# A hybrid decoder layer on one core: the merge takes the token chunks in the order 0, 1, 2 instead of 2, 0, 1, and the attention takes its token tiles in the order 0, 1, 2, 5, 4, 3, 7, 6

## The chip, the cores and the metric

The kernel runs on one core of one Trainium2 chip. The metric is the device time of one execution in microseconds (us), the median of several runs. Three runs of the kernel before gave 1844.86, 1845.64 and 1847.42 us.

## What is computed

One layer over 1024 prompt tokens and 8 sample tokens, with 1024 channels, everything in float32. The part that matters here is its second half, cut from the reference:

```python
# oa: output of the gated delta rule (mixer A); qb, kb, vb: queries, keys, values of mixer B
logits = einsum(qg, k_sel) * HD_B ** -0.5         # 8 query heads, 2 groups of keys and values
p  = softmax(where(valid, logits, -inf))          # at most 256 keys for each query, causal
ob = einsum(p, v_sel)
mix = sigmoid(ga) * (oa @ w_out_a) + sigmoid(gb) * (ob @ w_out_b)
h   = x + mix @ w_o
hn  = rms_norm(h, norm2_g)
y   = h + square(relu(hn @ w_up)) @ w_down
```

The first half (projections, delta rule, the choice of keys, the sample tokens' attention) stands ahead of it and is the same in both kernels.

## The kernel before, in words

The tokens are cut in two ways. The dense products work on three **chunks**: chunk 0 is token tiles 0 to 2 (384 columns), chunk 1 is tiles 3 to 5 (384 columns), chunk 2 is tiles 6 and 7 and the 8 sample tokens (264 columns). The attention works on eight **tiles** of 128 tokens, each in two groups `n` of four heads. Tile t looks at t + 1 blocks of 128 keys, so tile 0 has one block of work and tile 7 has eight.

Activations lie with channels on partitions. A dense product with one block of weights is a unit of 12 matmuls (four blocks of 128 input channels, three products each, since both operands are kept as a high and a low part), or 24 where two weight blocks feed one output. A block `wc` is 256 KB: SyncE (SP) issues its load, ScalarE writes its high part, VectorE (even number) or GpSimd (odd number) its low part.

`rest()` runs six chains side by side, and a scheduler turns them into one fixed order of instructions on each engine:

- The logit chain takes the groups (tile, n) in the order of the list `groups`: load of `q3`, rotation (`ro`, `qr`), transposition by TensorE (`ptq`), split into `qS`, logits `pat` by TensorE, VectorE's mask and maximum (`lg`, `st`), ScalarE's exponential. It is at most two groups ahead of the value chain.
- The value chain transposes for each group the reciprocal sums (`prr`) and the probabilities (`ptp`), splits them into `ph` (ScalarE) and `pl` (VectorE), multiplies with the values into `po`, and writes the scaled result `rb` to `obd` in DRAM.
- The merge chain first runs `mix_a` (the product with `w_out_a` for all three chunks, which doesn't need the attention), then `merge([j])` for each chunk j in `FIRST`, each as soon as the chunk's tiles are done, and last the merge of `REST`. A merge loads `ob` from `obd` (tiles `ld`), runs 8 units with `w_out_b` (`pdn<-ob`; VectorE makes `gb` and `ga`, ScalarE and GpSimd split the result into `mix`), then 8 units of 24 matmuls with `w_o` (`pdn<-mix`; VectorE adds into `hT`).
- The pool chain waits for all tiles and for the last `mix` of `FIRST`, closes the attention's buffers and opens those of the last stage; only then can the merge of `REST` begin, and `hn`, `ssq` and the root (`rst`, `rs`) of the chunks in `FIRST`.
- The MLP chain begins behind the merge of `REST`, and takes the chunks in the order `FIRST + REST`.

In the kernel before `FIRST, REST = [2, 0], [1]`: the two large tiles 7 and 6 are attended to first, beside `mix_a`; then tiles 0, 1, 2, while chunk 2 is merged; then tiles 5, 4, 3, while chunk 0 is merged; and chunk 1 is the `REST` whose merge stands alone ahead of the MLP.

Of the kernel before, what the change touches and what calls it, by code (L numbers as in the profile page):

```python
# [27 lines left out]
C_AQ, C_AZ, C_AB, C_BQ, C_BK, C_IQ, C_IK, C_GA = 0, 1536, 2048, 2056, 2568, 2824, 3336, 3408  # L28
WB = (5, 4)
LG = 9  # L30
FIRST, REST = [2, 0], [1]
XO = (0, 1, 2, 3, 4, 5, 6, 7, 8)
KVO = ([0, 1], [2, 3], [4, 5], [6, 7], [8])
IQO = (2, 3, 4, 5, 6, 7, 8)
# [12 lines left out]
class Event:  # L47
    t = None
# [80 lines left out]
def program(ctx, tc, I, O, dbg=None, upto=99):  # L129
# [1459 lines left out]
    def rest():  # L1589
# [12 lines left out]
        G.affine_select(cmask[:, P:], cmask[:, P:], pattern=[[-1, P]], compare_op=OP.is_ge, fill=NEG, base=0,  # L1602
                        channel_multiplier=1)
        chunks = FIRST + REST
        groups = [(t, n) for t in (7, 6, 0, 1, 2, 5, 4, 3) for n in range(2)]
        ev_lg, ev_pv = {g: Event() for g in groups}, {g: Event() for g in groups}
        front = {}

# [162 lines left out]
    if upto > 3:  # L1771
        rest()
# [80 lines left out]
```

## Time and profile before

| | before |
|---|---|
| median of 3 runs | 1845.64 us (1844.86 to 1847.42) |
| profiled execution, own time | 1847.76 us |
| its span in the trace | 1845.6 us |
| mean granted TensorE clock | 0.985 |
| TensorE matmul busy | 1767.7 us, 96% |
| VectorE, ScalarE, GpSimd busy | 1082.6, 813.0, 633.9 us |
| attention, mix_a and merges | about 794 to 1121 us of the span |
| MLP | 1121 to 1842 us |

The span is the time in the trace from the first to the last instruction. The profiled execution's own time is 2.2 us longer than its span, and 2.1 us above the median of the runs. Busy times are those of the matmuls as the profile models them.

### The profile page before, as it was taken

The numbers are of one execution on the slowest core, as the hardware profiler recorded it, in microseconds if no ns is written. First come the engines' busy times: TensorE is split into PE (matmuls) and PEld (weight loads), VectorE is DVE, ScalarE is ACT, GpSimd is POOL, SyncE is SP. The second block draws the span as 40 slices with busy tenths as digits, with TensorE's granted clock in tenths as the row PEclk, the third lists the DMA queues.
The fourth block names the chain that finished last, engine by engine and source line by source line (L and its number), as shares of the span: only waits on it lengthen the run. The fifth ranks groups of instructions, "written<-read, shape, count | busy, mean of one in ns | idle before, by whom it ended". The sixth has DMA issues, their size and how long they took to land. (4 is left out here: it accounts for less than half of the span.)

```text
span 1845.6 us, 32353 instructions
## 1 busy us (share of the span) xinstructions
PE 1767.7 (96%) x11796; PEld 1702.1 (92%) x11796; DVE 1082.6 (59%) x2871; ACT 813.0 (44%) x1865; POOL 633.9 (34%) x774
## 2 busy tenths in 40 slices
PE   6998979899999998989899989999999999999999
PEld 6998979789998998979789889999999999999999
DVE  8777767998889797358889685223232323231322
ACT  5456665465688542246677544222213131313130
POOL 5433235712332345231453665221212131213130
PEclk9999989999999998999999999999999999999999
DMA  6434463314443452663564552111111111111112
GB/s 215 130 106 153 141 216 108 92 56 119 135 149 113 147 166 87 199 219 115 177 173 139 179 159 86 52 41 52 46 51 48 46 47 46 46 52 41 52 29 93
DMA packets 160143, 199.27 MB, mean 108 GB/s; under 512 B 29648, under 2 KB 107464, under 8 KB 159976
## 3 DMA queue, kind: packets, MB, share of 16 engines
q1 hardware_dynamic: 155696, 183.57, 32.4%
q0 software_dynamic: 4288, 13.64, 2.5%
q8 instruction: 93, 1.52, 0.3%
q14 instruction: 66, 0.54, 0.1%
HBM read 149.51 MB, written 47.73 MB: 107 GB/s over the span
## 5 line engine op out<-in xcount | busy, mean ns | idle before, releaser
L86 PE MATMUL pdn<-hn,wc 128*128 128x384 f32 (+1 forms) x2304 | 362.0, 319 | 0.0
L86 PE MATMUL pdn<-u,wc 128*128 128x384 f32 (+1 forms) x2304 | 361.3, 318 | 0.0
L86 PEld LDWEIGHTS pdn<-hn,wc 128*128 128x128 f32 x2304 | 360.4, 188 | 0.3
L86 PEld LDWEIGHTS pdn<-u,wc 128*128 128x128 f32 x2304 | 360.1, 188 | 0.0
L86 DVE TENSOR_TENSOR hT<-hT,pdn 128x384 f32<-128x384 f32 (+1 forms) x216 | 110.5, 512 | 248.4 <-PE pdn L86 245.6
L86 PE MATMUL pdn<-xn,wu 128*128 128x384 f32 (+1 forms) x1440 | 253.0, 329 | 1.4 <-ACT z L86 1.4
L86 PEld LDWEIGHTS pdn<-xn,wu 128*128 128x128 f32 x1440 | 229.6, 193 | 8.2 <-issue 3.8
L86 DVE SCALAR_TENSOR_TENSOR r<-pdn,rs 128x384 f32<-128x384 f32 (+1 forms) x96 | 49.4, 516 | 273.5 <-PE pdn L86 273.4
L86 POOL TENSOR_TENSOR u<-r,u 128x384 fp32r<-128x384 f32 (+1 forms) x96 | 89.9, 937 | 274.9 <-ACT u L86 248.3
L86 PE MATMUL pa<-xn,wu 128*128 128x384 f32 (+1 forms) x864 | 157.7, 330 | 0.3 <-ACT a L86 0.3
L86 PEld LDWEIGHTS pa<-xn,wu 128*128 128x128 f32 x864 | 139.8, 193 | 2.7 <-ACT a L86 0.9
L86 ACT ACTIVATE r<-r 128x384 f32<-128x384 f32 (+1 forms) x96 | 47.1, 492 | 174.0 <-DVE r L86 173.3
L86 ACT ACTIVATE jka<-sc,nf 128x512 bf16<-128x512 f32 (+3 forms) x124 | 101.4, 820 | 37.8 <-DVE nf L86 26.7
L86 PE MATMUL pdn<-mix,wc 128*128 128x384 f32 (+1 forms) x576 | 95.0, 321 | 8.1 <-ACT mix L86 3.7
L86 PEld LDWEIGHTS pdn<-mix,wc 128*128 128x128 f32 x576 | 90.4, 188 | 11.8 <-ACT mix L86 4.5
L86 DVE SCALAR_TENSOR_TENSOR a<-u,cw,a 128x384 f32<-128x384 f32 (+1 forms) x108 | 73.3, 679 | 9.7 <-ACT a L86 8.4
L86 POOL TENSOR_TENSOR wu<-wu_4r,wu 128x512 fp32r<-128x512 f32 x32 | 41.7, 1303 | 89.7 <-ACT wu L86 83.3
L86 DVE TENSOR_SCALAR_CACHE_REDUCE jk<-sc,cf 128x768 bf16<-128x768 f32 (+1 forms) x62 | 66.3, 1072 | 1.5 <-ACT jka L86 1.5
L86 DVE SCALAR_TENSOR_TENSOR sc<-rl,wsg,sc 128x512 f32<-128x512 f32 (+1 forms) x70 | 51.3, 734 | 13.9 <-ACT rl L86 12.7
L86 PE MATMUL pqb<-wbq,xn 128*128 128x256 f32 (+1 forms) x432 | 59.3, 287 | 0.0
L86 PE MATMUL pdn<-oa,wc 128*128 128x384 f32 (+1 forms) x288 | 52.1, 329 | 7.0 <-DVE ga L86 6.5
L86 PEld LDWEIGHTS pqb<-wbq,xn 128*128 128x128 f32 (+1 forms) x432 | 55.2, 183 | 3.4
(888 smaller groups left out, 3234.2 us busy)
## 6 DMA issues: line engine op xcount, KB each, us to landing
wu_0r<-in_w_un SPq DMA_DIRECT2D x32, 256.0 KB
wu_4r<-in_w_un SPq DMA_DIRECT2D x32, 256.0 KB
gd<-g SPq DMA_DIRECT2D x32, 192.0 KB
ga<-gd SPq DMA_DIRECT2D x32, 192.0 KB
cqd<-a SPq DMA_DIRECT2D x24, 192.0 KB
xt<-in_x_prompt SPq DMA_DIRECT2D x8, 512.0 KB
obd<-rb SPq DMA_DIRECT2D x16, 256.0 KB
kvd<-kvt SPq DMA_DIRECT2D x8, 384.0 KB
```

The source lines that it names most:

```text
L86: return f(*a, **k)
```

## The change

Two lines. The first sets which chunks are merged beside the attention and which one is left for the end; the second sets the tiles' order so that each chunk's tiles are done when its merge is due.

```diff
-FIRST, REST = [2, 0], [1]
+FIRST, REST = [0, 1], [2]
...
         chunks = FIRST + REST
-        groups = [(t, n) for t in (7, 6, 0, 1, 2, 5, 4, 3) for n in range(2)]
+        groups = [(t, n) for t in (0, 1, 2, 5, 4, 3, 7, 6) for n in range(2)]
```

What the lines do to the order of instructions shows at three places. The first is TensorE's order where the attention begins, behind the first four units of `mix_a` (`pdn<-oa`: a unit of `mix_a`; `ptq`, `pat`, `prr`, `ptp`, `po`: the attention). Before:

```order
L86 MATMUL ptq<-ident,qr 128x128 x2
L86 MATMUL pdn<-oa,wc_10473 128x384 x12
L86 MATMUL pat<-kv,qS 128x512 x16
L86 MATMUL ptq<-ident,qr 128x128 x2
L86 MATMUL pdn<-oa,wc_10473 128x384 x12
L86 MATMUL pat<-kv,qS 128x512 x4
L86 MATMUL pdn<-oa,wc_10463 128x264 x12
L86 MATMUL prr<-ident,st 128x128 x4
L86 MATMUL ptp<-ident,lg 128x128 x8
L86 MATMUL pat<-kv,qS 128x512 x6
```

After the change the same place reads:

```order
L86 MATMUL ptq<-ident,qr 128x128 x2
L86 MATMUL pdn<-oa,wc_10475 128x384 x12
L86 MATMUL pat<-kv,qS 128x128 x8
L86 MATMUL ptq<-ident,qr 128x128 x2
L86 MATMUL pat<-kv,qS 128x128 x2
L86 MATMUL prr<-ident,st 128x128 x4
L86 MATMUL ptp<-ident,lg 128x128 x4
L86 MATMUL pat<-kv,qS 128x128 x6
L86 MATMUL ptq<-ident,qr 128x128 x2
L86 MATMUL po<-ph,kv 128x512
L86 MATMUL pdn<-oa,wc_10475 128x384 x12
L86 MATMUL po<-pl,kv 128x512
```

Tile 7's sixteen matmuls of 512 columns for one group have become tile 0's eight of 128 columns, and two units of `mix_a` that stood among the first two groups have moved behind them.

The second place is TensorE's order behind the last value product (`po`) of the attention. Before, seven pairs of units of 128x384 of chunk 0's `w_o` product follow it, fourteen units, of which eleven are shown:

```order
L86 MATMUL po<-pl,kv 128x512
L86 MATMUL pdn<-mix_12664,wc_13218 128x384 x12
L86 MATMUL pdn<-mix_12665,wc_13285 128x384 x12
L86 MATMUL pdn<-mix_12664,wc_13290 128x384 x12
L86 MATMUL pdn<-mix_12665,wc_13377 128x384 x12
L86 MATMUL pdn<-mix_12664,wc_13382 128x384 x12
L86 MATMUL pdn<-mix_12665,wc_13448 128x384 x12
L86 MATMUL pdn<-mix_12664,wc_13453 128x384 x12
L86 MATMUL pdn<-mix_12665,wc_13510 128x384 x12
L86 MATMUL pdn<-mix_12664,wc_13515 128x384 x12
L86 MATMUL pdn<-mix_12665,wc_13587 128x384 x12
L86 MATMUL pdn<-mix_12664,wc_13592 128x384 x12
```

After the change five pairs are left (of chunk 1), and then the merge of `REST` begins, on 264 columns:

```order
L86 MATMUL po<-pl,kv 128x512
L86 MATMUL pdn<-mix_12693,wc_13373 128x384 x12
L86 MATMUL pdn<-mix_12694,wc_13439 128x384 x12
L86 MATMUL pdn<-mix_12693,wc_13444 128x384 x12
L86 MATMUL pdn<-mix_12694,wc_13505 128x384 x12
L86 MATMUL pdn<-mix_12693,wc_13510 128x384 x12
L86 MATMUL pdn<-mix_12694,wc_13574 128x384 x12
L86 MATMUL pdn<-mix_12693,wc_13579 128x384 x12
L86 MATMUL pdn<-mix_12694,wc_13632 128x384 x12
L86 MATMUL pdn<-mix_12693,wc_13637 128x384 x12
L86 MATMUL pdn<-mix_12694,wc_13707 128x384 x12
L86 MATMUL pdn<-ob,wc_13712 128x264 x6
```

Four units of 128x384 have moved from behind the attention's end to ahead of it, and the sixteen outputs of the `REST` merge are 264 columns wide instead of 384.

The third place is SP's queue behind the last write of the attention's result (`obd<-rb`), with the loads of `ob` for `REST` (`ld<-obd`), of the residual (`hT<-in_xT`) and of weights (`wc`). Before:

```order
L1672 DMA obd<-rb 512x1x128
L216 DMA wc52r<-in_w_o 128x512
L216 DMA wc53r<-in_w_o 128x512
L216 DMA wc56r<-in_w_b 128x512
L1529 DMA ld<-obd 64x2x384 x2
L216 DMA wc50r<-in_w_o 128x512
L229 DMA hT_14009<-in_xT 128x1536 x2
L216 DMA wc54r<-in_w_o 128x512
L216 DMA wc55r<-in_w_o 128x512
L216 DMA wc57r<-in_w_b 128x512
L216 DMA wc58r<-in_w_b 128x512
L1529 DMA ld<-obd 64x2x384 x2
```

After the change:

```order
L1672 DMA obd<-rb 512x1x128
L216 DMA wc56r<-in_w_b 128x512
L1529 DMA ld<-obd 64x2x256
L216 DMA wc57r<-in_w_b 128x512
L1529 DMA ld<-obd 64x2x256 x3
L1532 DMA ld<-obs 128x2x8
L229 DMA hT_13979<-in_xT 128x1056 x2
L1529 DMA ld<-obd 64x2x256 x2
L1532 DMA ld<-obs 128x2x8
L216 DMA wc58r<-in_w_b 128x512
L216 DMA wc60r<-in_w_b 128x512
L1529 DMA ld<-obd 64x2x256 x2
```

The loads of `ob` stand closer behind the last write, with fewer loads of weights between them, and two small loads of the sample tokens' part (`obs`) have joined them.

## Rows read from the trace of the kernel before

**Rows 1.** The page's part 1: busy us, share of the span, instructions.

```profile
PE 1767.7 (96%) x11796; PEld 1702.1 (92%) x11796; DVE 1082.6 (59%) x2871; ACT 813.0 (44%) x1865; POOL 633.9 (34%) x774
```

**Rows 2.** Busy time by stretch: from:to, length, engines' busy us, PEclk, DMA share, GB/s.

```profile
809.30:825.00 15.70, 14.99 (x76) 11.49 (x77) 12.34 (x36) 9.88 (x17) 5.00 (x8) 1.00 0.73 242
825.00:896.00 71.00, 71.00 (x466) 65.84 (x465) 57.92 (x150) 44.26 (x96) 10.78 (x15) 1.00 0.43 130
896.00:925.00 29.00, 22.67 (x159) 19.97 (x158) 25.84 (x64) 19.87 (x52) 16.46 (x19) 1.00 0.65 192
925.00:964.00 39.00, 37.42 (x264) 33.59 (x263) 33.80 (x85) 27.41 (x59) 20.98 (x20) 1.00 0.65 183
964.00:1027.00 63.00, 63.00 (x409) 58.26 (x407) 53.95 (x123) 43.51 (x93) 22.93 (x20) 1.00 0.47 141
1027.00:1121.10 94.10, 84.42 (x461) 81.18 (x461) 75.54 (x98) 47.79 (x96) 65.98 (x51) 0.98 0.53 167
1130.00:1842.20 712.20, 712.18 (x4555) 711.86 (x4553) 195.42 (x355) 170.51 (x314) 169.40 (x158) 1.00 0.16 49
```

**Rows 3.** TensorE's waits, 896 to 925 us: us in total, times, longest.

```profile
PE pdn L86 <- DVE ga L86: 2.7, 1, 2.7
PE pat L86 <- DVE qS L86: 1.9, 2, 1.4
```

**Rows 4.** TensorE's waits, 1027 to 1121.1 us.

```profile
PE pdn L86 <- ACT mix L86: 3.7, 2, 2.0
...
PE pdn L86 <- ACT ob L86: 2.0, 1, 2.0
```

**Rows 5.** VectorE's groups by form, 873 to 925 us: count, busy us, mean ns, idle before.

```profile
L86 DVE TENSOR_TENSOR qS<-ptq,qS 64x256 fp32r<-64x256 f32 x11 | 4.7, 423 | 0.9 <-ACT qS L86 0.6
L86 DVE TENSOR_TENSOR ro<-q,tab 128x128 f32<-128x128 f32 x10 | 4.2, 446 | 0.2
...
L86 DVE TENSOR_TENSOR qr<-qr,ro 128x256 f32<-128x256 f32 x5 | 4.1, 819 | 0.1
...
L86 DVE CUSTOM_DVE_ANT_0 lg<-pat,cmask 128x128 f32<-128x128 f32 x8 | 2.2, 284 | 1.2 <-PE pat L86 1.2
```

**Rows 6.** ScalarE's groups by form, 873 to 925 us.

```profile
L86 ACT ACTIVATE qS<-ptq 64x256 fp32r<-64x256 f32 x10 | 3.7, 373 | 2.3 <-DVE qS L86 2.3
...
L86 ACT ACTIVATE lg<-lg,st 128x128 f32<-128x128 f32 x8 | 3.2, 399 | 0.4 <-DVE st L86 0.3
```

**Rows 7.** TensorE's timeline: start us, us, and the run of matmuls.

```profile
947.05 3.08 PE L86 MATMUL pdn<-mix,wc 128*128 128x264 f32 x24
...
1094.35 17.88 PE L86 MATMUL pdn<-mix,wc 128*128 128x384 f32 x101 [1.66 <-ACT mix L86]
```

**Rows 8.** VectorE's waits, 1027 to 1121.1 us.

```profile
DVE hT L86 <- PE pdn L86: 10.4, 6, 3.7
DVE ob L86 <- ACT ob L86: 6.1, 2, 3.3
```

**Rows 9.** VectorE's groups by form, 1027 to 1121.3 us.

```profile
L86 DVE SCALAR_TENSOR_TENSOR hn<-hT,g,hn 128x384 fp32r<-128x384 f32 x15 | 16.5, 1100 | 0.5 <-ACT hn L86 0.5
...
L86 DVE TENSOR_TENSOR ga<-ga,gb 128x384 f32<-128x384 f32 x8 | 7.5, 940 | 0.0
...
L86 DVE TENSOR_TENSOR wc<-wc56r,wc 128x512 fp32r<-128x512 f32 x1 | 1.5, 1500 | 0.0
...
L86 DVE TENSOR_TENSOR wc<-wc54r,wc 128x512 fp32r<-128x512 f32 x1 | 0.7, 693 | 0.2 <-ACT wc L86 0.2
```

**Rows 10.** The timeline's end: VectorE's last two additions into hT.

```profile
1838.03 0.43 DVE L86 TENSOR_TENSOR hT<-hT,pdn 128x264 f32<-128x264 f32 x1 [0.89 <-PE pdn L86]
...
1842.22 0.56 DVE L86 TENSOR_TENSOR hT<-hT,pdn 128x384 f32<-128x384 f32 x1 [1.55 <-PE pdn L86]
```

**Rows 11.** Busy time in stretches of 5 us around two of TensorE's waits; columns as in rows 2.

```profile
895.00:900.00 5.00, 2.30 (x18) 2.05 (x17) 2.76 (x9) 2.79 (x10) 2.15 (x3) 1.00 0.61 170
...
1065.00:1070.00 5.00, 4.67 (x18) 4.67 (x19) 3.77 (x4) 2.24 (x5) 4.96 (x4) 0.66 0.39 132
```

## The prediction

> **What bounds the kernel now.** The page's busy shares come first: TensorE's matmuls fill 96% of the span, VectorE 59%, GpSimd 34% [rows 1]. A change of order removes no matmul, so it can only move the other 4%, and only in the stretches whose order differs. I looked for these with busy times by stretch [rows 2]. The MLP, 712 us long, has 0.02 us of idle TensorE; it takes the same units in another order of chunks, so I count it as unchanged. The attention and the merges show three kinds of stretch. From 825 to 896 us (tiles 7 and 6 beside `mix_a`) and from 964 to 1027 us (tiles 5, 4, 3 beside merges) TensorE has no idle time at all. From 896 to 925 us, tiles 1 and 2 with few units beside them, it idles 29.00 − 22.67 = 6.3 us, while VectorE is busy 25.84 of 29 us; from 925 to 964 us another 1.6 us. And from the attention's end at 1027 us to the MLP at 1121 us it idles 94.10 − 84.42 = 9.7 us. The waits name the causes: in 896 to 925 us VectorE's `ga` (2.7 us) and `qS` (1.9 us) [rows 3]; behind the attention the last parts of `mix` (3.7 us) and of `ob` (2.0 us) [rows 4]. The reader is to see that a tile of few key blocks gives TensorE little to do and VectorE nearly as many instructions as a large tile, and that a merge without attention beside it waits for VectorE and what follows on it.
>
> **Start: the small tiles meet an empty pipeline.** Before, the attention starts on tile 7, and 809 to 825 us shows 0.7 us of idle time [rows 2]. After the change the order puts tile 0's groups there, eight matmuls of 128 columns each, and two units of `mix_a` move behind them. Go through TensorE's new order. Behind the first group's `pat` it has only a `ptq` until the second group's `qS` is made. That takes VectorE two `ro`, one `qr` and one `qS`, 2 × 0.45 + 0.82 + 0.42 = 2.1 us [rows 5], and ScalarE's half of `qS`, 0.37 us [rows 6], about 2.5 us together. The first `prr` then needs the group's last exponential, 0.40 us [rows 6], and VectorE's reciprocal behind it; with `prr` of the second group I put 0.6 us on each, 1.2 us. The third group's `ptq` needs four `lg` of 0.28 us and the two `ro` and the `qr`, 1.1 + 1.7 = 2.8 us [rows 5], of which the transpositions and six `pat` between cover about half: 1.4 us. Two `po` wait for their `pl`, as an estimate 0.5 us each. Sum 6.1 us, less the 0.7 us of before: **+5.4 us**. The lower bound: VectorE and ScalarE begin a group early enough that only the 2.1 us for the first `qS` remain, +1.4. The upper: tiles 0, 1 and 2 idle throughout as in 896 to 925 us, 0.22 us per us over some 45 us, +9.
>
> **Middle: the old holes close.** Tiles 5, 4, 3, 7, 6 now run beside the rest of `mix_a` and the merges of chunks 0 and 1. Both old stretches in which large tiles had merge units beside them show zero idle time [rows 2], so the 6.3 and 1.6 us go; I leave 1.5 us for new joints: **−6.4 us**, bounds −7.9 (all) and −2.4 (5.5 us remain, as the tail end of tile 2 is still short of cover).
>
> **End: a shorter cover.** TensorE's matmuls from the last value product to the MLP become fewer: four units of 12 on 384 columns move ahead of it, and 288 matmuls (96 of `w_out_b`, 192 of `w_o`) go from 384 to 264 columns. One of 384 takes 17.88 / 101 = 0.177 us, one of 264 takes 3.08 / 24 = 0.128 us [rows 7]. That is 48 × 0.177 + 288 × 0.049 = 22.6 us less there. None of it is a gain: the narrow units of chunk 2 and the wide ones of chunk 1 have changed places, and that work now stands beside the attention. If the idle time stayed at 9.7 us the stretch would be 94.1 − 22.6 = 71.5 us.
>
> VectorE's work hardly shrinks. It is 75.54 us there now [rows 2]. Two additions into `hT` go (2 × 0.56), sixteen `hT` and `gb` shrink by 0.56 − 0.43 = 0.13 us each, 2.1 us [rows 10], eight `ga` shrink in proportion to the columns, 7.5 × 120 / 384 = 2.3 us [rows 9]; two low parts of weights (1.5 us each, the dearer row) go, 3.0 us, two parts of `ob` give 0.5 us, and one more `hn` comes, 1.1 us [rows 9]. Net −7.9: 67.6 us. Its idle time there is 94.10 − 75.54 = 18.6 us, of which 10.4 us are waits for TensorE's `hT` units and 6.1 us waits for `ob` [rows 8]. The first kind is slack that goes when TensorE has less to do. If all the rest stays, 8.2 us, the stretch is 67.6 + 8.2 = 75.8 us, 4.3 us more idle TensorE than now. If the waits for `ob` go too, since its loads stand closer behind the last `obd` in SP's new queue, VectorE alone asks for 69.7 us, less than the 71.5 above: −1.8. I take **+3.0**, nearer the upper end, because the shorter cover (ten units, 10 × 12 × 0.177 = 21.2 us) must hold the write, the loads, the addition and both parts of `ob`, and fifteen `hn` of 1.1 us stand on VectorE in the same stretch.
>
> The price of VectorE's work there is not fixed. A low part of a weight block takes 0.69 us in one row and 1.50 in another of the same stretch, and `ga` takes 0.94 us [rows 9], while GpSimd is busy 65.98 of 94.10 us [rows 2]. The Trainium skill, GPSIMD Engine Reference, section Specifications, says that GpSimd's SBUF interfaces are shared with VectorE, with contention where VectorE reads two inputs from SBUF; these two rows agree, and by that rule the same GpSimd work in a shorter stretch would make VectorE's instructions dearer still. As a term it is bounded by rows: if the seventeen low parts and the sixteen `hn`, by the row of 1.1 us, become dearer by a fifth, that is 33 × 1.2 × 0.2 = 8 us on VectorE, and the end costs +11 instead of +3.
>
> **Tail.** The last unit is now one of 264 columns; its addition is 0.13 us shorter [rows 10]: −0.1 us.
>
> **Sum.** +5.4 − 6.4 + 3.0 − 0.1 = +1.9 us. The profiled execution's own time is 1847.76 us (span 1845.6), 2.1 us over the median of the runs, so the changed kernel would take 1849.7 us in such an execution and 1845.64 + 1.9 = **1847.5 us** as a median. A measurement here can tell about 0.2% (3.7 us) from no change, so this is a small loss that may not be seen.
>
> **Rivals.**
>
> *The end gets cheaper (faster, 0.17).* The wider merge of chunk 1 was what GpSimd and VectorE collided over; the narrow one collides less, and the fifteen or so low parts whose price lies near 1.5 us fall to the row of 0.69 us [rows 9]. That frees 15 × 0.81 = 12 us of VectorE, which then asks for 64 us, and TensorE, the bound again, idles about 4 us for the first `ob` and `mix` instead of 9.7: −5.7 in place of +3.0, sum −6.8, about 1838.8 us. For it: 0.69 occurs in this stretch. Against: GpSimd's share rises. It decides as soon as the mean low part costs less than about 0.9 us.
>
> *The end gets dearer (slower, 0.16).* The contention above, +11: sum +9.9, about 1855.5 us.
>
> *TensorE's clock falls between short bursts (slower, 0.14).* In 1065 to 1070 us, behind a wait of 2.0 us, the granted clock is 0.66, between its levels of 1.2 and 2.4 GHz; in 895 to 900 us, with a wait of 2.7 us in it, it stays 1.00 [rows 11]. A stretch of 5 us at 0.66 loses 5 × 0.34 = 1.7 us. If the start and the end, with more such waits, show four more of these, the sum is +1.9 + 6.8 = +8.7, about 1854.3 us. The Trainium skill, TensorE: Matmul & The Clock Gate, section HAM oscillation — how this bites in real kernels, describes this: bursts that are short against the waits between them start cold each time. The first row agrees with it, the second does not, hence the small chance.
>
> *The middle stays (slower, 0.11).* Tile 2 and the first large tiles find `mix_a`'s units spent by the small tiles, and only 2 of the 7.9 us go: sum +1.9 + 4.4 = +6.3, about 1851.9 us.
>
> **Chances and range.** The forecast has 0.42, spread from −5 to +5 us: 0.37 of it within 0.2% and 0.05 faster than that. Faster: 0.17 + 0.05 = 0.22. Within 0.2%: 0.37. Slower: 0.16 + 0.14 + 0.11 = 0.41. The forecast's own range is 1841 to 1851 us; the range of 8 in 10 takes in all of the slower cases but the far end and half of the faster one: 1839.5 to 1857 us.
>
> **What the new profile would show.** Right: in the first 25 us behind tile 0's first `pat`, 5 to 7 us of TensorE waits for `qS`, `st` and `pl`; from there to the last value product less than 2 us; then about 60 us of matmuls in a stretch of some 74 us, with waits for `mix` or `ob`, and VectorE busy over 90% of it. Wrong: an idle start as short as before (then the small tiles are covered and the sum turns negative), an end with idle time under 6 us or over 18, a granted clock under 0.9 over either stretch, or an MLP with idle time of its own.

## The result, and the profile after

The changed kernel takes 1859.29 us (median of 5 runs, 1857.16 to 1860.16) where the kernel before takes 1847.42 us on the same chip (5 runs, 1844.86 to 1851.11): 1.0063 times the time, 95% interval 1.0052 to 1.0073. That is 11.9 us slower. The forecast said 1.9 us, and the time lies above its range, which ended at 1857 us.

Busy time by stretch of the changed kernel, in the columns of [rows 2]; the attention's first tile starts at 809.4 us, its last value product ends at 1057 us, the MLP begins at 1133.2 us:

```profile
809.40:845.00 35.60, 32.46 (x188) 29.36 (x188) 27.73 (x90) 20.76 (x62) 10.06 (x15) 0.90 0.64 206
845.00:882.00 37.00, 36.77 (x237) 33.93 (x235) 28.22 (x76) 20.63 (x45) 8.38 (x9) 1.00 0.65 178
882.00:892.40 10.40, 5.16 (x21) 4.67 (x22) 6.05 (x12) 4.78 (x10) 5.92 (x6) 0.67 0.29 92
892.40:1057.00 164.60, 161.75 (x962) 149.80 (x961) 127.47 (x280) 102.59 (x199) 57.81 (x51) 0.99 0.46 133
1057.00:1133.20 76.20, 62.50 (x404) 58.80 (x403) 70.37 (x90) 42.03 (x88) 58.44 (x47) 0.96 0.53 159
1142.00:1854.10 712.10, 712.10 (x4567) 712.10 (x4566) 206.04 (x358) 165.64 (x315) 171.15 (x158) 1.00 0.16 49
```

The MLP is as long as before. Idle TensorE time is 3.1 us at the start (0.7 before), 0.2 + 5.2 + 2.9 = 8.3 us from there to the last value product (7.9 before), and 13.7 us behind it (9.7 before): 6.9 us more in all. And there is a second part that no idle time shows. From the first unit of `mix_a` to the MLP, TensorE does the same matmuls in both kernels (a few of their records are missing from each trace), but is busy longer:

```profile
794.06:1121.10 327.04, 304.45 (x1878) 279.89 (x1877) 268.00 (x567) 198.06 (x422) 151.44 (x143) 0.99 0.55 168
```

```profile
791.78:1133.20 341.42, 311.86 (x1869) 288.54 (x1868) 270.58 (x564) 197.79 (x419) 150.81 (x141) 0.96 0.53 158
```

The first row is the kernel before, the second the changed one: 7.4 us more busy time, at a mean granted clock of 0.96 instead of 0.99. The stretch as a whole is 14.4 us longer; ahead of it, where both kernels do the same, this profile of the changed kernel is 2.3 us shorter (the first unit of `mix_a` starts at 791.78 us instead of 794.06). Where the added busy time is spent shows in stretches of 5 us of the changed kernel, and in TensorE's timeline there:

```profile
815.00:820.00 5.00, 5.00 (x18) 4.50 (x18) 2.89 (x11) 2.62 (x10) 1.34 (x2) 0.50 0.78 263
...
885.00:890.00 5.00, 2.76 (x11) 2.46 (x12) 3.71 (x8) 3.44 (x8) 4.21 (x6) 0.55 0.30 95
...
1070.00:1075.00 5.00, 5.00 (x22) 5.00 (x21) 5.00 (x5) 2.97 (x7) 5.00 (x5) 0.68 0.34 88
1105.00:1110.00 5.00, 4.31 (x23) 4.10 (x24) 5.00 (x10) 2.92 (x6) 3.56 (x4) 0.73 0.49 148
```

```profile
812.26 0.44 PE L86 MATMUL pat<-kv,qS 128*128 128x128 f32 x2 [1.47 <-DVE qS L86]
813.34 0.73 PE L86 MATMUL prr<-ident,st 128*128 128x128 f32 x4 [0.64 <-DVE st L86]
...
816.96 4.01 PE L86 MATMUL pdn<-oa,wc 128*128 128x384 f32 x12
...
879.70 2.26 PE L86 MATMUL pdn<-oa,wc 128*128 128x384 f32 x12
887.24 1.12 PE L86 MATMUL prr<-ident,st 128*128 128x128 f32 x4 [5.28 <-DVE st L86]
```

A unit of `mix_a` that takes 2.26 us at 879.70 us takes 4.01 us at 816.96 us, in a stretch whose clock is 0.50, the lower of the two levels; ahead of it TensorE had waits of 1.47 and 0.64 us and short matmuls. The longest single wait, 5.28 us, is new: `prr` waits for `st` at 887.24 us. ScalarE's and VectorE's timelines say for what:

```profile
877.90 0.94 ACT L86 ACTIVATE ob<-ld 128x384 fp32r<-128x384 f32 x2 [1.20 <-issue]
885.12 0.94 ACT L86 ACTIVATE ob<-ld 128x384 fp32r<-128x384 f32 x2 [6.28 <-POOL ld L86]
885.97 0.92 ACT L86 ACTIVATE lg<-lg,st 128x768 f32<-128x768 f32 x1
```

```profile
885.68 0.78 DVE L86 TENSOR_TENSOR ob<-ld,ob 128x384 fp32r<-128x384 f32 x1 [6.66 <-ACT ob L86]
887.01 0.18 DVE L86 RECIPROCAL st<-st 128x4 f32<-128x4 f32 x1 [0.55 <-ACT lg L86]
```

ScalarE stands still 6.28 us in front of the second half of chunk 0's `ob`, which GpSimd has not added up yet. The last two loads of this half are issued behind other transfers at 877.63 us, and the addition starts at 883.29 us (timelines of SyncE and GpSimd):

```profile
877.63 1.23 SPq L1529 DMA_DIRECT2D ld<-obd  x2
883.29 1.80 POOL L86 TENSOR_TENSOR ld<-ld 128x768 f32<-128x768 f32 x1 [5.30 <-issue]
```

GpSimd is idle for 5.30 us ahead of it, and the profile names no releaser there; that it waits for these loads is read from the order of the program. Behind that `ob`, in the fixed order, wait the last exponential of tile 5's group and then VectorE's reciprocal, on which `prr` waits. ScalarE's orders (listed, without times) show the place. In the kernel before, the two halves stand apart, with attention work between them:

```
L86 ACTIVATE ob<-ld 128x264 x2
L86 ACTIVATE lg,st<-lg,st 128x256
L86 ACTIVATE wc_11633<-wc11r 128x512
L86 ACTIVATE qS<-ptq 64x2x128 x2
L86 ACTIVATE wc_11677<-wc12r 128x512
L86 ACTIVATE rb<-prr 128x512
L86 ACTIVATE ph<-ptp 128x512 x2
L86 ACTIVATE ob<-ld 128x264 x2
```

In the changed kernel all four conversions stand in a row, ahead of an exponential:

```
L86 ACTIVATE lg,st<-lg,st 128x768
L86 ACTIVATE ob<-ld 128x384 x4
L86 ACTIVATE lg,st<-lg,st 128x768
L86 ACTIVATE ph<-ptp 128x512
```

Behind the attention the waits are VectorE's low parts of weights first, then `mix` and a high part of a weight block; VectorE is busy 70.37 of 76.20 us there, and the wait for `hT` that led its idle time before is gone:

```profile
PE pdn L86 <- DVE wc L86: 5.3, 4, 2.3
PE pdn L86 <- ACT mix L86: 3.2, 2, 1.9
PE pdn L86 <- ACT wc L86: 2.9, 1, 2.9
```

### The profile page after: what moved, and what is told of

Same layout as the page of the kernel before. It is cut to its first block, busy times and chain, and to the rows that moved or that the text cites. A ratio compares the mean times of both kernels' runs of the same rounds, so it can differ in the third digit from the quotient of the medians.

```text
span 1857.5 us, 32361 instructions
## 1 busy us (share of the span) xinstructions
PE 1774.7 (96%) x11796; PEld 1710.0 (92%) x11796; DVE 1099.7 (59%) x2871; ACT 808.0 (44%) x1865; POOL 638.3 (34%) x774
## 4 chain that ended last, share of the span: by engine, by line
PE 47%; DVE 3%; issue 1%; POOL 1%; DMA 1%; ACT 0%; SPq 0%; DVEq 0%; ACTq 0%; POOLq 0%
PE pdn L86 43%; PE po L86 1%; PE ptp L86 1%; PE pat L86 1%; DVE hn L86 1%; DVE rst L86 0%; DMA ld<-obd 0%; DVE wc L86 0%; POOL ld L86 0%; PE prr L86 0%; DVE hT L86 0%; DVE rs L86 0%; DVE ga L86 0%; POOL ssq L86 0%; DVE gb L86 0%
## 5 line engine op out<-in xcount | busy, mean ns | idle before, releaser
L86 PE MATMUL pdn<-mix,wc 128*128 128x384 f32 (+1 forms) x576 | 98.9, 328 | 12.2 <-DVE wc L86 3.7
L86 DVE SCALAR_TENSOR_TENSOR sc<-rl,wsg,sc 128x512 f32<-128x512 f32 (+1 forms) x70 | 52.9, 757 | 11.6 <-ACT rl L86 10.5
L86 ACT ACTIVATE lg<-lg,st 128x128 f32<-128x128 f32 (+7 forms) x64 | 49.4, 773 | 21.6 <-DVE st L86 21.4
```

What stands on the lines that cost most here:

```text
L86: return f(*a, **k)
```

## Experiments

Each time is a median, taken on the same chip as runs of the kernel before; ratios are to those runs, with their 95% interval. The chip differs from one group of experiments to the next, so across groups ratios are compared and not times. Four things were to be told apart: the tiles' order at the start, the narrow `REST` at the end, the wait at the loads of `ob`, and the clock.

**Start alone, end alone.**

```diff
-FIRST, REST = [0, 1], [2]     # tiles 0, 1, 2, 5, 4, 3, 7, 6
+FIRST, REST = [0, 2], [1]     # e_start: tiles 0, 1, 2, 7, 6, 5, 4, 3
+FIRST, REST = [1, 0], [2]     # e_end:   tiles 5, 4, 3, 0, 1, 2, 7, 6
```

> Small tiles first as in the change, but chunk 1 stays REST, so the end is the old one (FIRST = [0, 2], REST = [1], tiles 0, 1, 2, 7, 6, 5, 4, 3). Theory 1, the loss has two parts (about 7 us between the first tile and the last value product, about 5 us in the merge behind it): 1847.4 + 7 = 1854 us, with the wait for st of some 5 us at the loads of chunk 0's ob and the low clock at the start in the trace, and the end at about 94 us with 10 us idle. Theory 2, the narrow REST is the cause: within 2 us of the kernel before, 1847 us. Theory 3, the order of the tiles is the cause alone: 1857 to 1860 us.

> Chunk 2 as REST as in the change, but large tiles first (FIRST = [1, 0], REST = [2], tiles 5, 4, 3, 0, 1, 2, 7, 6). Theory 1: start as before, end as in the changed kernel, 1847.4 + 5 = 1852 us, with under 1 us idle in the first 16 us of the attention and 13 to 14 us idle behind the last value product. Theory 2: 1857 to 1860 us. Theory 3: about 1847 us.

Measured: e_start 1863.83 us (1.0091, 1.0073 to 1.0108), e_end 1852.78 us (1.0029, 1.0017 to 1.0041), beside 1847.28. Stretches of e_start, then of e_end (first tiles; to the last value product; to the MLP):

```profile
810.90:846.00 35.10, 32.15 (x207) 29.84 (x206) 26.95 (x87) 20.81 (x63) 9.96 (x14) 0.95 0.64 198
846.00:1053.30 207.30, 197.51 (x1248) 182.34 (x1246) 160.20 (x374) 127.08 (x259) 70.19 (x69) 0.98 0.48 141
1053.30:1136.60 83.30, 66.61 (x365) 62.89 (x364) 68.78 (x89) 42.01 (x87) 58.80 (x47) 0.92 0.55 166
```

```profile
808.60:846.60 38.00, 34.29 (x204) 30.84 (x205) 31.55 (x83) 23.28 (x46) 8.30 (x12) 0.96 0.55 183
846.60:1039.20 192.60, 185.31 (x1127) 170.39 (x1127) 154.11 (x369) 122.58 (x265) 66.20 (x65) 0.99 0.51 148
1039.20:1128.90 89.70, 79.22 (x497) 75.74 (x497) 75.23 (x101) 48.68 (x100) 67.09 (x54) 0.94 0.55 166
```

e_end came out at the 1852 us of theory 1, but not for its reason: it idles 3.7 us in the first tiles, where under 1 us was expected, and 10.5 us at the end, where 13 to 14 us were. So the narrow `REST` costs only 0.8 us of idle time when a longer cover stands ahead of it. e_start, slower than each of the three theories said, refutes theory 1: the old `REST` did not bring the old end back (16.7 us idle, at a clock of 0.92), and in the middle TensorE waits 6.57 us for a `ph` that stands behind `ob` in ScalarE's order (its timeline):

```profile
885.07 0.94 ACT L86 ACTIVATE ob<-ld 128x384 fp32r<-128x384 f32 x2 [11.16 <-POOL ld L86]
```

Neither is the start's order the whole of it, since e_start is slower than the change. The parts do not add: an order sets by its own places what comes late.

**Clock at the start.**

```diff
+pw = 512 if t < 2 else cn
-pa = pst("pat", "pa")[:, :cn]
+pa = pst("pat", "pa")[:, :pw]
...                                    # the matmuls cover pw columns, VectorE reads cn
```

> The changed kernel with the logits of tiles 0 and 1 computed over 512 keys instead of 128 and 256 (the extra columns are not used), which adds matmul columns at the start, about 4 us of TensorE work, part of it inside waits. Theory A, the granted clock falls at 815 to 820 us because TensorE has too little to do: the clock stays at 1.00 there, the unit that took 4.0 us takes 2.3, and the time is 1857 to 1860 us although work was added. Theory B, the waits between alone decide: the clock falls as before and the time rises by 2 to 4 us to 1861 to 1863 us.

Measured: 1858.10 us (1.0062, 1.0047 to 1.0076). The first tiles:

```profile
808.90:843.40 34.50, 32.50 (x200) 29.23 (x199) 27.79 (x89) 20.75 (x62) 9.91 (x14) 1.00 0.66 208
```

Clock 1.00, where the same start without the added columns has 0.90 in each of five profiles (the change twice, e_newton, e_fill, e_obpool), and a time within the interval of the change's although work was added. That speaks for theory A, but it is one profile, the idle time in it is shorter too (2.0 us against 3.1), the loads of `ob` fell elsewhere in this order, and e_ld4 below, with narrow matmuls and a start that differs little, also shows 1.00. So it is not settled.

**Buffers for the loads of `ob`.**

```diff
-r  = w([P, 2, CM], "ld", bufs=3, pool=cur["L"])
+r  = w([P, 2, CM], "ld", bufs=4, pool=cur["L"])   # e_ld4, b_ld4; e_ld2: 2 until the last stage
...                                                # the same for the tile lo; with 4 also for the last stage's spare
```

> The changed kernel with four buffers for the tiles ld instead of three. Theory A, the wait of 5.3 us for st at 882 us comes from the fourth load of chunk 0's ob, which waits for a buffer and then holds ScalarE's and VectorE's queues: the wait falls below 2 us and the time from 1859.3 to about 1853 to 1855 us. Theory B, VectorE is late there with its own work whatever the loads do: the wait stays over 4 us and the time within 1.5 us of 1859.3.

> The changed kernel with two buffers instead of three for the tiles ld of the attention stage (three stay for the REST merge). Theory A (the load of chunk 0's ob, waiting for a buffer, holds ScalarE's and VectorE's queues): the wait at about 882 us grows by 2 to 4 us, the time is 1861 to 1864 us. Theory B (VectorE is late there whatever the loads do): within 1.5 us of 1859.3.

> The kernel before with four buffers for the tiles ld. If the load of ob held the queues there as well (the 6.3 us idle from 896 to 925 us is behind VectorE, and ob of chunk 2 is loaded in that stretch), 1841 to 1844 us; if the waits there come from the small tiles' short work alone, within 1.5 us of 1847.3.

Measured: e_ld4 1853.46 us (1.0037, 1.0022 to 1.0052), e_ld2 1854.21 us (1.0046, 1.0028 to 1.0063), b_ld4 1856.59 us (1.0061, 1.0044 to 1.0078). With four buffers the wait of 5.3 us became one of 2.8 us (theory A said under 2) and, by the ratios, 0.26% or 4.8 us came back, the time that theory A said; but with two buffers no wait over 0.5 us is left in that place and the time is 0.17% or 3.1 us lower, where it said 2 to 4 us worse. The two intervals overlap, so the gain may be noise, but the loss that theory A said is not there. So the number of buffers is not the cause. What goes with the wait in these kernels is how long ScalarE stands in front of `ob`: 11.16 us in e_start, 6.28 and (second profile, below) 3.84 us in the change, 5.05 in e_ld4, with TensorE waits of 6.57, 5.28, 2.84 and 2.79 us behind it; and in e_ld2, where the second half stands nine rows of other work behind the first (ScalarE's timeline),

```profile
890.22 0.94 ACT L86 ACTIVATE ob<-ld 128x384 fp32r<-128x384 f32 x2 [0.92 <-POOL ld L86]
```

and TensorE has no wait there. The profile of e_ld2 also shows that the two parts of the loss come apart: from the first unit of `mix_a` to the MLP the busy time is that of the kernel before, while the idle time, 27.5 us, stays near that of the change (29.6 us), in other waits. This profiled execution, 1850.54 us, is the fastest of its six.

```profile
793.78:1125.55 331.77, 304.23 (x1878) 281.61 (x1877) 271.89 (x565) 197.03 (x419) 148.82 (x141) 0.99 0.53 164
```

b_ld4 is a miss: the same edit costs the kernel before 0.61%, 11 us. Its idle time rises by 3.5 us and its busy time by 6.4 us over the same matmuls; why just there stays open.

**`ob` out of the attention's queues.**

```diff
-split(out[:, 0, k + x], out[:, 1, k + x], r[:, x], "act", "pool" if x else "dve")
+on = name == "ob" and j == FIRST[0]
+split(out[:, 0, k + x], out[:, 1, k + x], r[:, x], "pool" if on else "act",
+      "pool" if x or on else "dve")       # and copy("pool", ...) on GpSimd
```

> The changed kernel with both parts of chunk 0's ob made by GpSimd alone, so that the loads of ob no longer stand in ScalarE's and VectorE's queues among the attention's instructions; GpSimd gets about 6 us more work there. Theory A, corrected (not the number of buffers but the place of ob's four conversions in ScalarE's order, all four in a row ahead of an exponential, makes the wait of 5.3 us at 882 us): that wait is gone, TensorE's idle time from the first tile to the last value product falls from 11.5 to 6 to 8 us, the time from 1859.3 to 1853 to 1856 us. Theory B (VectorE is late with its own work): the wait stays over 3 us and the time within 1.5 us of 1859.3. If GpSimd's qr becomes late instead, a wait for qS of 2 us or more appears in the groups behind it and the gain is half.

Measured: 1850.36 us (11 runs) beside 1848.22 us (23 runs), 1.0009 (0.9999 to 1.0019); the change itself was run again beside it:

> The changed kernel once more, unchanged, for a second profile. If the low clock belongs to the order, the granted clock falls again behind the same waits (815 to 825, 885 to 895, 1070 to 1075, 1105 to 1110 us) and TensorE's busy time between the first unit of mix_a and the MLP is again 6 to 8 us over that of the kernel before; if it is chance, the places and the sum differ by more than 4 us. Time 1857 to 1861 us.

Measured: 1858.51 us (1.0059, 1.0047 to 1.0071). Stretches of e_obpool, then of a_again:

```profile
812.90:847.70 34.80, 31.95 (x184) 28.63 (x184) 27.21 (x90) 20.68 (x62) 10.14 (x14) 0.90 0.68 211
847.70:1040.10 192.40, 190.39 (x1147) 173.95 (x1146) 156.24 (x359) 120.35 (x243) 70.57 (x68) 0.99 0.51 143
1040.10:1127.70 87.60, 75.33 (x486) 72.14 (x486) 72.55 (x97) 45.16 (x93) 59.79 (x49) 0.96 0.52 158
```

```profile
811.60:847.00 35.40, 32.42 (x188) 29.30 (x188) 27.84 (x91) 20.82 (x62) 9.72 (x14) 0.90 0.68 216
847.00:1055.40 208.40, 202.53 (x1214) 187.16 (x1213) 159.88 (x367) 127.81 (x254) 72.44 (x66) 0.98 0.48 138
1055.40:1132.30 76.90, 63.76 (x404) 60.17 (x404) 74.06 (x93) 42.85 (x91) 59.25 (x47) 0.94 0.54 162
```

With `ob` out of the two queues the wait is gone, the middle idles 2.0 us instead of 5.9 (a_again) or 8.3 us (first profile), no long wait for GpSimd's `qr` takes its place, and nearly all of the loss comes back (0.09% is left of 0.59%, 9 us, where 3 to 6 us were expected). VectorE's own work was not late: theory B falls. The edit also reorders what follows (six more units stand behind the last value product), so the 9 us are the wait and what its removal does to the rest. They are not the clock, as far as this profile shows: from the first unit of `mix_a` to the MLP TensorE idles 21.4 us, 1.2 us less than in the kernel before, but is busy 6.8 us longer, nearly as long as in the change. The profiled execution, 1853.18 us, is the slowest of the 11. That stretch in e_obpool, then in a_again:

```profile
795.01:1127.65 332.64, 311.21 (x1879) 287.03 (x1877) 266.12 (x562) 193.15 (x413) 151.07 (x145) 0.97 0.55 163
```

```profile
793.80:1132.30 338.50, 312.19 (x1869) 288.95 (x1868) 272.03 (x567) 198.48 (x422) 151.79 (x141) 0.96 0.54 161
```

a_again shows that the low clock belongs to the order: busy 312.19 us, 7.7 us over the kernel before, with granted clocks of 0.52, 0.69, 0.78 and 0.66 in the 5 us from 815, 885, 1065 and 1105 us. The wait for `st` was 2.8 us this time.

**The end.**

```diff
-        for _ in range(3):      # steps of the root, second normalisation
+        for _ in range(1):      # e_newton
...
+            for i in range(6):  # e_fill: ahead of each REST unit, overwritten
+                T.matmul(p[:, :CN[j]], ws[i % 4][:, 0], fill, start=True, stop=True)
```

> The changed kernel with one step instead of three in the iteration for the root of the second normalisation (two steps of each chunk's rs are left out, so the normalisation is less exact). That takes about 9 us of VectorE's work out of the stretch between the last value product and the MLP, and none of TensorE's, GpSimd's or the DMA queues'. Theory D, VectorE's fixed order bounds that stretch: the stretch falls from 76.3 us to 70 to 72 us and the time from 1859.3 to 1853 to 1856 us. Theory S, the weights' and ob's supply bounds it: the stretch stays within 1.5 us and the time within 2 us.

> The changed kernel with 96 throwaway matmuls of 264 columns, six ahead of each unit of the REST merge (16 units), overwritten by the unit's first product; 96 x 0.128 = 12.3 us of TensorE work, none elsewhere. Theory D (VectorE bounds the stretch behind the attention, TensorE's 13.7 us of idle time and its time at a low clock are slack there): the stretch grows by 0 to 4 us, the clock in it rises to 0.98 or more, the time is 1859 to 1863 us. Rival, TensorE bounds it: the stretch grows by 10 to 12 us and the time to about 1870 us.

Measured: e_newton 1854.19 us (1.0042, 1.0026 to 1.0057), e_fill 1859.18 us (1.0068, 1.0051 to 1.0084). The stretch behind the last value product, e_newton, then e_fill:

```profile
1061.00:1133.30 72.30, 63.37 (x404) 60.03 (x404) 63.62 (x78) 42.28 (x89) 57.76 (x47) 0.93 0.54 169
```

```profile
1058.30:1138.80 80.50, 72.25 (x509) 69.84 (x509) 73.30 (x93) 43.19 (x91) 57.97 (x48) 0.98 0.51 159
```

Taking 70.37 − 63.62 = 6.8 us of work from VectorE shortens the stretch by 3.9 us and, by the ratios, the time by as much (0.21%, with intervals that just overlap); adding 12.3 us of matmuls lengthens it by 4.3 us, with a higher clock, and leaves the total where it was. So VectorE bounds the end, though not alone, since 3.9 of the 6.8 us come back; TensorE has some 8 us to spare there.

**Was the old hole the same wait, and is there a better order?**

```diff
-FIRST, REST = [0, 1], [2]     # tiles 0, 1, 2, 5, 4, 3, 7, 6
+FIRST, REST = [2, 1], [0]     # c_210: tiles 7, 6, 5, 4, 3, 2, 1, 0
                               # c_obpool: that, and ob of the first merged chunk by GpSimd
                               # b_obpool: the kernel before, and ob of the first merged chunk by GpSimd
```

> Large tiles first, small tiles last, with a wide chunk as REST: FIRST = [2, 1], REST = [0], tiles 7, 6, 5, 4, 3, 2, 1, 0. If the loss comes from small tiles that meet no units beside them and from a narrow REST, this order has neither (small tiles beside chunk 1's merge, REST of 384 columns): start as before with 0.7 us idle, middle under 3 us idle, 1841 to 1846 us. If what costs is rather where the fixed orders let an ob, mix or weight block come late, whatever the tiles: 1847 to 1856 us.

> The kernel before with both parts of its first merged chunk's ob (chunk 2) made by GpSimd alone. Theory A: 2.7 of the 6.3 us idle between 896 and 925 us, the wait for ga, was this queue too and not the small tiles (VectorE's ob stood ahead of ga); it goes, idle time from the first tile to the last value product falls from 8.6 to 5 to 6 us, the time by 2 to 5 us to about 1843 to 1845 us. Theory T (the small tiles alone made it): the idle time stays within 1.5 us and the time within 2 us of the kernel before.

> The order 7, 6, 5, 4, 3, 2, 1, 0 with FIRST = [2, 1], REST = [0], and the first merged chunk's ob made by GpSimd alone. Its wait of 2.2 us for ga at 906 us goes by theory A: 1840 to 1843 us, under the 1844.7 us of that order alone; by theory T the same as that order, 1843 to 1846 us.

Measured: c_210 1844.69 us beside 1848.22 (0.998, 0.9972 to 0.9989), b_obpool 1847.70 and c_obpool 1844.82 us beside 1846.98 (1.0007, 0.9995 to 1.0019; 0.9990, 0.9979 to 1.0001). c_210 beats both kernels, by a little; its stretches:

```profile
812.50:847.00 34.50, 33.77 (x199) 28.44 (x198) 29.76 (x77) 22.41 (x40) 6.09 (x9) 1.00 0.52 158
847.00:1023.00 176.00, 169.13 (x1133) 156.47 (x1131) 151.15 (x373) 119.06 (x270) 67.12 (x68) 0.98 0.53 151
1023.00:1118.00 95.00, 88.70 (x486) 85.31 (x485) 77.24 (x101) 49.60 (x99) 67.66 (x54) 0.98 0.57 179
```

It starts as the kernel before, idles 6.9 us in the middle, more than the 3 us that were expected, and 6.3 us at the end, where it gains. In the trace of the kernel before, VectorE's `ob` also stands ahead of the `ga` on which TensorE waits 2.7 us:

```profile
898.70 0.43 DVE L86 TENSOR_TENSOR ob<-ld,ob 128x264 fp32r<-128x264 f32 x1 [1.90 <-ACT ob L86]
...
899.05 0.42 DVE L86 TENSOR_TENSOR ga<-pdn,ga 128x264 f32<-128x264 f32 x1
```

b_obpool takes this wait down to 0.4 us, and yet its time and its idle sum (8.9 us in place of 8.6) stay: waits for `st`, `ga`, `ph` and `qS` of the small tiles, 0.6 to 1.7 us each, take its place. c_obpool is no faster than c_210 either: its wait of 2.2 us for `ga` is gone, but the wait for `hT` is 5.5 us instead of 3.4, and one of 1.6 us for GpSimd's `q` is new. So theory A names the wait rightly and theory T the time.

## Why the prediction was wrong, point by point

- **What bounds the kernel, and the MLP:** right. The MLP is as long as before, and the loss arises between the first unit of `mix_a` and the MLP.
- **Start, +5.4 us:** too large as idle time; it measured +2.4 us (3.1 against 0.7). The first wait was the one forecast, for `qS`, 1.47 us instead of 2.5; the third group's `ptq` was covered.
- **Middle, −6.4 us:** this step failed. The old holes beside the small tiles did close, but a new wait came with chunk 0's merge, 5.3 us (2.8 in the second profile), at `ob` in ScalarE's queue: +0.4 us in the first profile, −2.0 us in the second. The prediction looked at `ob` only behind the attention. With `ob` out of the queues the middle idles 2.0 us, near the 1.5 us that the step left for it (e_obpool, with six units moved behind the attention). And the 2.7 us of [rows 3] were read as the small tiles' alone, where `ob` stood in the queue too.
- **End, +3.0 us:** near: +4.0 and +3.5 us of idle time in the two profiles. The reason was right (VectorE busy 70.4 us, forecast 67.6; e_newton, e_fill), the waits named were in part others: low parts of weights (5.3 us) ahead of `mix` (3.2 us). Neither rival on their price came: VectorE's low parts there take 1.1 us on average in both kernels (19 before, 16 after). The cheaper end's "fifteen or so" near 1.5 us were read out of one row; 5 of the 19 lie above 1.4 us.
- **The clock, +0 in the sum:** the second failed step, and the largest term. The sum took every matmul at its rate at full clock; 7.4 and 7.7 us of added busy time were measured. The rival had the mechanism and nearly the price (four more places of 1.7 us, 6.8 us; the slices of 5 us show five from the first tile on, and one before), but got a chance of 0.14, since one of two old rows showed no fall [rows 11].
- **Where the clock falls:** argued, in part. It falls to 0.50 in the 5 us from 815 us (0.52 in the second profile), behind small matmuls with waits between, and to 0.55 in those from 885 us (0.69). The Trainium skill, TensorE: Matmul & The Clock Gate, HAM oscillation — how this bites in real kernels, tells of a wait behind which the next burst of matmuls starts at the low clock. The fall at 885 us, behind 5.28 us of waiting, agrees with that; but at 815 us it falls behind waits of only 1.47 and 0.64 us, while it stays at 1.00 behind 1.47 us at the same place in e_ld4 and behind the 2.7 us of [rows 11]. The prediction's other row does not show short bursts either: over 18 us of matmuls stand ahead of its wait of 2.0 us.
- **How much the clock costs:** open, in part. The mean clock of whole runs says the same as the busy time, though it counts idle time too: on one chip it is 0.9854 in 23 runs of the kernel before and 0.9815 in 6 of the changed one (a_again); 0.0039 of 1858 us is 7.2 us. Shown is that the clock goes with these orders and that filling the end raises it there (e_fill); that each fall is made by the wait ahead of it is argued from the rows, and no run changes the clock alone, so its share of the 11.9 us stays open: e_obpool gives back 9 us with nearly all of the added busy time still in its profile.
- **Sum of the terms as measured:** +2.4 + 0.4 + 4.0 + 7.4 = +14.2 us for the profiled execution (341.42 − 327.04 = 14.4, less the 2.3 us ahead of `mix_a`), +2.3 − 2.0 + 3.5 + 7.7 = +11.5 for the second; +11.9 in the medians.

## What to carry to other kernels

When a change of order is priced, follow every instruction that waits on a load in the queues of the engines that serve other work; the cost is what stands behind it in that fixed order, not the load. A wait on TensorE can have a second price, the matmuls behind it at the lower clock (0.50 behind the waits at the start here, but 1.00 behind the 2.7 us of [rows 11]), so several short waits belong in the sum and not among the rivals. An order is more than its parts: undoing one half of this change made it slower than the whole, so a good order is found by running candidates and reading the stretch where each loses.

## What the runs showed of the hardware that was not expected

The added busy time, at a lower clock, was as large as the added idle time (7.4 against 6.9 us). A change of buffers alone, meant to relieve one load, moved the time by +11 us in one kernel and −5 us in the other; the order of instructions changed with it, and what in b_ld4's order costs the 11 us was not found.
